# The first load of an average-pooling kernel, in three transfers by partitions

## The chip, the cores and the metric

The kernel runs on one core of a Trainium2 chip. The metric is the device time of one execution in microseconds (us), as the median of several runs. Of the core's engines the kernel uses VectorE (DVE in the profile) for all arithmetic and SyncE (SP) to issue transfers. Transfers are carried by the 16 DMA engines of the core. GpSimd (POOL) only fills a few constants at the start.

## The reference

The input `x` is a float32 array of shape (8, 32, 32, 32, 32): batch, channels, depth, height, width. The result is the mean of each 2 x 2 x 2 window, an array of shape (8, 32, 16, 16, 16). Cut to what matters:

```python
for i in range(out_d):
    for j in range(out_h):
        for k in range(out_w):
            window = x[:, :, 2*i:2*i+2, 2*j:2*j+2, 2*k:2*k+2]
            result[:, :, i, j, k] = np.mean(window, axis=(-3, -2, -1))
```

Every input value is read once: 33.55 MB in, 4.19 MB out.

## The kernel before

Batch and channel make 256 rows of 32,768 values. The first 128 rows are the first half of the work (`t == 0`), one row on each of the 128 partitions. The other 128 rows are the second half (`t == 1`), which is taken as flat memory and cut so that each load is one contiguous region.

`plan` lists ten units: four of 32 KB a partition (4.19 MB each) in the first half, then four of 24 KB and two of 16 KB in the second. For each unit the loop at the end of `pool_rows` takes a tile `tin` from a pool of five buffers, issues its load on SP (line 87) and calls `pool_unit`. There VectorE adds pairs of depth planes (line 68), pairs along the width (line 71) and pairs along the height with the factor 0.125 (line 74), which goes into one of two output buffers `obuf`. Since there are five buffers, the load of unit six waits until VectorE is through with unit one, and so on. [...]

Three stores follow: the first four units of the second half, the whole first half, and the last two units. All stand on SP's queue behind the ten loads.

The second function works on the finished list of instructions. It rewrites the source patterns of the loads of the second half into 64 rows of double length, and those of two stores; the loads of the first half stay as they are, 128 rows with a distance between them. It relaxes the wait of the first store by moving it one VectorE instruction later. Then it takes the first transfer in the list and moves it into the opening block, ahead of the barrier in which all engines meet at the start:

```python
    load = next(i for i in program if isinstance(i, mybir.InstDMACopy))
    ...
    program.remove(load)
    opening.insert(barrier, load)
```

The rest of it rewrites the end of the program, so that SP and not the barrier waits for the semaphores of the stores. A transfer is known to have landed by its semaphore; the framework gives out eight of them to the transfers in turn, and VectorE's first addition of a unit waits for the semaphore of that unit's load.

Of the kernel before, what the change touches and what calls it, by code (L numbers as in the profile page):

```python
# [12 lines left out]
@with_exitstack  # L13
def pool_rows(
    ctx: ExitStack,
    tc: tile.TileContext,
    x: bass.AP,
    kernel_size: int,
    out: bass.AP,
):  # L20
    nc = tc.nc
    assert kernel_size == 2, "only kernel_size == 2 supported"

    B, C, D, H, W = x.shape
    P = nc.NUM_PARTITIONS
    assert (B * C, D, H, W) == (2 * P, 32, 32, 32)
    add = mybir.AluOpType.add

    xv = x.rearrange("b c d h w -> (b c) (d h w)")[:P]
    ov = out.rearrange("b c d h w -> (b c) (d h w)")[:P]
    xf = x.rearrange("b c d h w -> (b c d h w)")[P * 128 * KF:]
    of = out.rearrange("b c d h w -> (b c d h w)")[P * 16 * KF:]

    pool_in = ctx.enter_context(tc.tile_pool(name="pin", bufs=5))
    pool_out = ctx.enter_context(tc.tile_pool(name="pout", bufs=1))
    obuf = [pool_out.tile([P, 16 * KF], F32, name=f"obuf{t}") for t in range(2)]
    dummy = pool_out.tile([P, 1], F32, name="dummy")


    plan = [
        (0, 0, 32),
        (0, 32, 32),
        (0, 64, 32),  # L50
        (0, 96, 32),
        (1, 0, 24),
        (1, 24, 24),
        (1, 48, 24),
        (1, 72, 24),
        (1, 96, 16),
        (1, 112, 16),
    ]

    def pool_unit(buf, t, k0, kb, split):  # L60

        od = kb // 8
        a = buf.rearrange("p (o dd e) -> p o dd e", o=od, dd=2)
        b = buf[:, :od * 1024]
        bv = b.rearrange("p (o e) -> p o e", o=od)
        cuts = (0, 1, od) if split else (0, od)
        for o0, o1 in zip(cuts, cuts[1:]):
            nc.vector.tensor_add(out=bv[:, o0:o1], in0=a[:, o0:o1, 0], in1=a[:, o0:o1, 1])  # L68
        bv = b.rearrange("p (e ww) -> p e ww", ww=2)
        c = buf[:, od * 1024:od * 1536]  # L70
        nc.vector.tensor_add(out=c, in0=bv[:, :, 0], in1=bv[:, :, 1])  # L71
        cv = c.rearrange("p (j hh k) -> p j hh k", hh=2, k=16)
        o0 = k0 * KF // 8
        nc.vector.tensor_tensor_reduce(  # L74
            out=obuf[t][:, o0:o0 + od * 256].rearrange("p (j k) -> p j k", k=16),
            in0=cv[:, :, 0], in1=cv[:, :, 1],
            scale=0.125, scalar=0.0, op0=add, op1=add, accum_out=dummy[:, :],
        )

    for t, k, kb in plan:  # L80
        tin = pool_in.tile([P, 32 * KF], F32, tag="tin", name="tin")
        buf = tin[:, :kb * KF]
        if t == 0:
            src = xv[:, k * KF:(k + kb) * KF]
        else:
            src = xf[P * k * KF:P * (k + kb) * KF].rearrange("(p e) -> p e", p=P)
        nc.sync.dma_start(out=buf, in_=src)  # L87
        pool_unit(buf, t, k, kb, split=k == 96 and t == 1)

    for k, n, kb in [(0, 4, 3), (12, 2, 2)]:
        nc.sync.dma_start(
            out=of[P * k * KF:P * (k + n * kb) * KF].rearrange("(u p e) -> p u e", u=n, p=P),
            in_=obuf[1][:, k * KF:(k + n * kb) * KF].rearrange("p (u e) -> p u e", u=n),
        )
        if k == 0:
            nc.sync.dma_start(out=ov, in_=obuf[0])


def kernel(tc: tile.TileContext, x: bass.AP, kernel_size: int, out: bass.AP):
    nc = tc.nc
    pool_rows(tc, x, kernel_size, out)
    tc.close()
    tc.compile()  # L105
# [123 lines left out]
```

## Time and profile before

| What | Value |
|---|---|
| median of 10 runs | 91.36 us (91.34 to 91.56) |
| the profiled execution | 91.39 us |
| its span, from the first to the last instruction of the program | 86.8 us |
| VectorE busy | 64.5 us, 74% of the span |
| data read and written | 33.55 MB and 4.19 MB |
| loads, stores | 10, 3 |

The span begins with the issue of the first load and ends with the last instruction that belongs to a line of the program. The last store lands after that, so the profiled execution's own time is longer than its span. In the lists below, times are microseconds from the start of the span unless they are marked as ns. L87 is line 87 of the kernel, `SPq` is SP's queue, and "idle before" names what ended an engine's idle time.

### The profile page before, as it was taken

Reading aid. Unit: us, or ns where it says so; the run is one execution under the profiler, and the core shown is the slowest. Engines: PE = TensorE matmul, PEld = TensorE weight load, DVE = VectorE, ACT = ScalarE, POOL = GpSimd, SP = SyncE. Lnnn points to the kernel's source line nnn. Section 1 sums busy time; section 2 is a strip of 40 time slices with the busy share of each in tenths; the row PEclk is TensorE's granted clock in tenths of the full one; section 3 lists DMA queues with packets and bytes.
Section 4 is the critical chain, followed back from the end, with each engine's and each line's share of the span. In section 5 each row is a group of like instructions: output and inputs, shape, how many; then the busy total and the mean of one; then the engine's idle time right before and its main releaser. Section 6 shows DMA issues by size and latency. Waiting matters only on the chain.

```text
span 86.8 us, 91 instructions
## 1 busy us (share of the span) xinstructions
DVE 64.5 (74%) x41; POOL 0.2 (0%) x4
## 2 busy tenths in 40 slices
DVE  0000049992999749992999999799589959999992
POOL 0000000000000000000000000000000000000000
DMA  8889997999979999699889988889988899889999
GB/s 242 378 363 468 483 483 332 393 483 483 483 332 393 483 483 483 302 423 604 363 363 408 657 385 363 363 363 589 499 363 363 363 483 483 378 347 423 431 446 415
DMA packets 1299, 36.75 MB, mean 424 GB/s; under 512 B 176, under 2 KB 176, under 8 KB 176
## 3 DMA queue, kind: packets, MB, share of 16 engines
q1 hardware_dynamic: 1299, 36.75, 99.3%
HBM read 33.55 MB, written 4.19 MB: 435 GB/s over the span
## 4 chain that ended last, share of the span: by engine, by line
DMA 71%; DVE 26%; issue 0%; SPq 0%; DVEq 0%
DMA tin<-in_x_dram 71%; DVE tin L68 14%; DVE tin L71 8%; DVE obuf L74 4%; SPq L87 0%; DVE dummy L74 0%; DVEq L105 0%
## 5 line engine op out<-in xcount | busy, mean ns | idle before, releaser
L68 DVE TENSOR_TENSOR tin<-tin 128x4096 f32<-128x4096 f32 (+3 forms) x11 | 35.9, 3260 | 20.0 <-DMA tin<-in_x_dram 20.0
L71 DVE TENSOR_TENSOR tin<-tin 128x2048 f32<-128x2048 f32 (+2 forms) x10 | 18.7, 1865 | 0.3
L74 DVE CUSTOM_DVE_ANT_1 obuf<-tin 128x1024 f32<-128x1024 f32 (+2 forms) x10 | 10.1, 1012 | 0.3
L74 DVE DVE_READ_ACCUMULATOR2_ANT dummy<- 128x1 f32 x10 | 0.8, 82 | 0.0
L210 POOL MEMSET const-uint8-127<- 128x1 uint8 x1 | 0.1, 102 | 0.0
L210 POOL MEMSET const-bfloat16-1.0<- 128x1 bf16 x1 | 0.1, 101 | 0.0
L210 POOL MEMSET const-float32-0.0<- 128x1 f32 x1 | 0.1, 98 | 0.2 <-issue 0.2
L210 POOL MEMSET const-float32-1.0<- 128x1 f32 x1 | 0.1, 98 | 0.0
## 6 DMA issues: line engine op xcount, KB each, us to landing
tin<-in_x_dram SPq DMA_DIRECT2D x4, 4096.0 KB, 25.7
tin<-in_x_dram SPq DMA_DIRECT2D x4, 3072.0 KB, 34.5
tin<-in_x_dram SPq DMA_DIRECT2D x2, 2048.0 KB, 25.4
out_dram<-obuf SPq DMA_DIRECT2D x1, 2048.0 KB, 10.3
out_dram<-obuf SPq DMA_DIRECT2D x1, 1536.0 KB, 6.1
out_dram<-obuf SPq DMA_DIRECT2D x1, 512.0 KB, 4.8
```

The costliest lines, as they stand in the source:

```text
L68: nc.vector.tensor_add(out=bv[:, o0:o1], in0=a[:, o0:o1, 0], in1=a[:, o0:o1, 1])
L71: nc.vector.tensor_add(out=c, in0=bv[:, :, 0], in1=bv[:, :, 1])
L74: nc.vector.tensor_tensor_reduce(out=obuf[t][:, o0:o0 + od * 256].rearrange("p (j k) -> p j k", k=16), in0=cv[:, :, 0], in1=cv[:, :, 1], s ...
L210: nc = _bacc.Bacc("TRN2", target_bir_lowering=False, num_devices=1)
```

## The change

The load of the first unit is issued as three transfers into the same tile: partitions 0, 4, 8, ..., 124 (32 of them), then 2, 6, 10, ..., 126 (32), then all the odd ones (64). All other loads stay one transfer of 128 partitions. The rewriting of the program is unchanged: it moves the first transfer of the list, which is now the first of the three parts. The other two parts stand behind the barrier, ahead of the load of unit two.

```diff
         else:
             src = xf[P * k * KF:P * (k + kb) * KF].rearrange("(p e) -> p e", p=P)
-        nc.sync.dma_start(out=buf, in_=src)
+        for a, step in ((0, 4), (2, 4), (1, 2)) if t == k == 0 else ((0, 1),):
+            nc.sync.dma_start(out=buf[a:P:step], in_=src[a:P:step])
         pool_unit(buf, t, k, kb, split=k == 96 and t == 1)
```

## The prediction

> **What bounds the kernel now.** I read the page first, then the timeline, then the transfers in a window over the first four microseconds. The page, its first line, its row for VectorE, its account of the transfers and its list of issues:
>
> ```profile
> span 86.8 us, 91 instructions
> ...
> DVE 64.5 (74%) x41; POOL 0.2 (0%) x4
> ...
> DMA  8889997999979999699889988889988899889999
> ...
> HBM read 33.55 MB, written 4.19 MB: 435 GB/s over the span
> ...
> out_dram<-obuf SPq DMA_DIRECT2D x1, 2048.0 KB, 10.3
> out_dram<-obuf SPq DMA_DIRECT2D x1, 1536.0 KB, 6.1
> out_dram<-obuf SPq DMA_DIRECT2D x1, 512.0 KB, 4.8
> ```
>
> To see: the 16 DMA engines are busy in every slice, VectorE three quarters of the time. 37.75 MB must pass. The last column is time from issue to landing. The timeline of the engines:
>
> ```profile
> 12.08 4.43 DVE L68 TENSOR_TENSOR tin<-tin 128x4096 f32<-128x4096 f32 x1 [12.08 <-DMA tin<-in_x_dram]
> ...
> 21.79 4.42 DVE L68 TENSOR_TENSOR tin<-tin 128x4096 f32<-128x4096 f32 x1 [1.69 <-DMA tin<-in_x_dram]
> ...
> 31.51 4.43 DVE L68 TENSOR_TENSOR tin<-tin 128x4096 f32<-128x4096 f32 x1 [1.70 <-DMA tin<-in_x_dram]
> ...
> 41.23 4.42 DVE L68 TENSOR_TENSOR tin<-tin 128x4096 f32<-128x4096 f32 x1 [1.70 <-DMA tin<-in_x_dram]
> ...
> 78.43 0.58 SPq L98 DMA_DIRECT2D out_dram<-obuf  x1
> ...
> 85.21 0.57 SPq L93 DMA_DIRECT2D out_dram<-obuf  x1
> ```
>
> Each unit starts when its load lands, and loads of 4.19 MB land 9.71 us apart: 432 GB/s. The second store, issued at 78.43, lands 10.3 later at 88.7; the last, issued at 85.21, lands 4.8 later at 90.0, that is 1.3 after the one ahead of it. Its 0.52 MB take 1.21 at 432 GB/s, so it queued behind the other and the engines stayed full. The time is therefore a start, then 37.75 MB at the engines' rate (87.4 us), then an end. The profiled execution took 91.39, of which 1.4 lie outside the first issue and the last landing. A change counts if it moves the first data, breaks the flow, or lowers the rate.
>
> The first load landed at 12.08, not 9.71: 2.37 us are the start. The transfers in the window from 0 to 4 us, in 40 slices of 0.1 us, a packet being counted where it begins:
>
> ```profile
> DMA  0000000000999090908000000008979990000000
> GB/s 0 0 0 0 0 0 0 0 0 0 2621 983 655 0 328 0 328 0 328 0 0 0 0 0 0 0 0 328 983 328 983 1966 655 0 0 0 0 0 0 0
> DMA packets 32, 1.05 MB, mean 262 GB/s; under 512 B 0, under 2 KB 0, under 8 KB 0
> ```
>
> 328 in a slice is one packet of 32,768 bytes. Nothing moves for 1.0 us. Then eight engines start in one slice, three, two, and the last three at 1.4, 1.6 and 1.8: mean 1.21 us. The second packets begin between 2.7 and 3.3, mean 3.05. So the first packet of an engine takes 1.84 on average, and 32,768 bytes on 16 engines at 432 GB/s should take 1.21. The excess is 0.63 us, and late starters lose little of it, since all engines reach their second packet together.
>
> [...]
>
> **The change part by part.** (a) The issue ahead of the barrier describes 32 rows instead of 128, so each engine's list is two long and not eight. [...] If the excess is the delay of the first reads, nothing is won. Bounds: 0 to 0.91 us gained. I take half the excess, 0.31, because the last three starters lost little although they too made their first read, so not all of it is a delay of every first read[...].
>
> (b) Two more issues on SP. The issues of the loads on SP's queue, durations in ns as least, median and most, and the waits beside them:
>
> ```profile
> L87 SPq DMA_DIRECT2D tin<-in_x_dram x10: 333/472/567, 0.0 to 55.3; - x10
> L87 SPq EVENT_SEMAPHORE  x5: 17/17/17, 12.1 to 49.8; - x5
> ```
>
> 2 x 0.47 = 0.94 us. Behind them stand loads two to five, issued in 0.78 to 2.72 now, then until about 3.7. Load two is first needed when load one is through the engines, near 11.7, so it keeps some 9 us of cover; without it each issue would cost its 0.47. Parts two and three are issued near 0.8 and 1.2. The first part feeds each engine with two packets, 1.84 + 1.21 from 1.21, to about 4.3. Part two had its own wait of 1.0 us over by 1.8 (the same wait as the first issue, an estimate), so 2.4 us of cover.
>
> (c) Each transfer ends with one more semaphore write per engine. The trace shows no gap of its own there: three consecutive pitches of 9.71 us include it. I put 0.01 us each, 0.02 in all; between 0 and 0.05.
>
> (d) VectorE's first add must wait for three semaphores, and load six, which reuses that buffer, too: at most two more waits of 17 ns on each engine. VectorE idles 1.7 us before each of the next three adds, so this is hidden; bare, it would be 0.03. SP's stands ahead of load six, which is held until 20.1 by VectorE anyway. Semaphores shift round the loads and stores, with no more of them at the end.
>
> (e) If the flow begins x earlier, each landing, the adds behind it and the stores move x earlier together. The last store is issued 3.5 us before the one ahead lands, so a delayed VectorE has over 1 us before the stream runs dry; that delay doesn't arise here.
>
> Sum on the profiled execution: 91.39 - 0.31 + 0.02 = 91.10. The median of the runs is 91.36, 0.03 less: 91.07.
>
> **The rivals.** *The start is latency.* The first packets take as long with two rows as with eight;[...] only 0.02 is added. For it: nothing moves for 1.0 us, most of which is after the issue's 0.375. Against it: late starters lose little. 91.38.
>
> [...] Place: the first 4.19 MB. At half rate they take 19.4 us instead of 9.7: 101.1, and all behind moves along[...]. It decides once these bytes flow below about 412 GB/s, 0.5 us lost. Against it: the later loads read 64 double rows and still run at full rate[...].
>
> *A wait for landing.* The parts interleave in one tile; if the program takes them as overlapping, part two is issued only when part one has landed and part three after that. Two restarts of 2.37 us: 91.38 + 4.7 = 96.1. It decides if one such wait stands on SP. I think interleaved rows are told apart.
>
> *Dry lists.* An engine that finishes its two packets before the next list has reached it pays the first-packet excess again, 0.3 to 1.3 us over two joints: 91.7 to 92.6. It decides if part two arrives after 4.3; the 2.4 us of cover in (b) speak against it.
>
> **How the numbers follow.** A difference up to 0.2%, 0.18 us, is about what measurement can't tell from none. The forecast 0.42 (90.5 to 91.18; its own range), latency 0.32, dry lists 0.09, wait 0.07[...]. Faster 0.42, same 0.32, slower 0.26. The range begins at 90.6, leaving 0.03 of the fast tail, and takes in the same and the dry lists up to 92.6: 0.80. [...]
>
> **What would show it.** Right: in the first 4 us the 16 first packets begin closer together and second packets before 2.7 on average; VectorE's first add at about 11.8, with pitches of 9.71 after it. Latency: first add at 12.1. Dry lists: a gap between 4 and 8 us. Wait: SP's second issue after 4.8. [...] The prediction is wrong if the first add moves later, or moves earlier and the last store doesn't.

## The result and the profile after

The changed kernel takes 92.83 us (median of 9 runs, 91.82 to 93.20) against 91.39 us for the kernel before on the same chip (31 runs, 91.32 to 91.56). From all these runs it is estimated to be 1.0146 times as long, 95% interval 1.0129 to 1.0162. The profiled execution took 92.69, that of the kernel before 91.39.

The page of the changed kernel, the rows that answer to those shown of the kernel before:

```profile
span 88.1 us, 95 instructions
...
DVE 64.5 (73%) x41; POOL 0.2 (0%) x4
...
DMA  7699998999979999979889988898889997996999
...
HBM read 33.55 MB, written 4.19 MB: 429 GB/s over the span
...
out_dram<-obuf SPq DMA_DIRECT2D x1, 2048.0 KB, 10.3
out_dram<-obuf SPq DMA_DIRECT2D x1, 1536.0 KB, 6.1
out_dram<-obuf SPq DMA_DIRECT2D x1, 512.0 KB, 4.8
```

VectorE works as long as before, the stores take as long from issue to landing, the bytes are the same. Only the span is longer, by 1.3. The timeline of the changed kernel says where:

```profile
13.52 4.43 DVE L68 TENSOR_TENSOR tin<-tin 128x4096 f32<-128x4096 f32 x1 [13.52 <-DMA tin<-in_x_dram]
...
23.12 4.43 DVE L68 TENSOR_TENSOR tin<-tin 128x4096 f32<-128x4096 f32 x1 [1.59 <-DMA tin<-in_x_dram]
...
32.83 4.42 DVE L68 TENSOR_TENSOR tin<-tin 128x4096 f32<-128x4096 f32 x1 [1.69 <-DMA tin<-in_x_dram]
...
86.50 0.57 SPq L97 DMA_DIRECT2D out_dram<-obuf  x1
```

The first add is late by 13.52 - 12.08 = 1.44 us. The second is late by 1.33, the third by 1.32, the last store by 86.50 - 85.21 = 1.29. All of the loss is there before the first unit is complete, and the rest of the kernel is the old one, moved. Of the 1.44 at the first add, 0.10 is VectorE's own: its wait for three semaphores is now partly an instruction by itself, at 13.42 in the trace, ahead of the add at 13.52. Since VectorE idles before the second add, this goes no further. The transfers of the changed kernel in the window from 0 to 4 us, 0.1 us a slice:

```profile
DMA  0000000000000999990990700000008999990000
GB/s 0 0 0 0 0 0 0 0 0 0 0 0 0 1311 655 983 655 328 0 655 328 0 328 0 0 0 0 0 0 0 328 655 983 1311 655 1311 0 0 0 0
```

The first packets begin at 1.3 instead of 1.0. The mean of the 16 starts, read from the slices as in the prediction, is 1.64 instead of 1.21; the last is at 2.2 to 2.3. That is the first part of the loss. The second shows in the window from 4 to 6 us, slices of 0.05 us, where a packet of 32,768 bytes counts 655:

```profile
GB/s 0 0 0 0 0 0 0 655 1311 1966 0 655 1311 655 655 1311 1311 0 0 0 0 0 655 0 0 0 0 0 0 0 0 0 1311 655 655 655 1311 1311 1311 655
DMA packets 44, 0.92 MB, mean 459 GB/s; under 512 B 16, under 2 KB 16, under 8 KB 16
```

The 16 small packets, of 4 bytes each, are the ends of part one, one an engine. Fifteen engines begin part two between 4.35 and 4.85. The sixteenth begins at 5.1. Between 5.6 and 6.1 the trace again has only fifteen starts, so the first packet of the late engine also took longer than the others'. The packet records don't name the engines, but only one end of part one, at 4.54, has no packet right behind it. So this engine stands idle for 0.6 us; then its first packet of part two takes 1.88 us, where most of the others take 1.2. The excess of some 0.65 is about that of a first packet at the start of the kernel.

The trace also keeps the 16 increments of each load's semaphore, one an engine. In the kernel before they come within 0.4 us of each other at every load, and so do those of part one here. Of part two, fifteen have come by 7.56 and the last comes at 8.52; of part three, by 12.42 and at 13.39; of the last load, by 80.61 and at 81.49. One engine falls behind where part two follows part one, and every later load waits for it.

SP's issues of the loads in the changed kernel:

```profile
L91 SPq DMA_DIRECT2D tin<-in_x_dram x12: 449/481/942, 0.0 to 56.7; - x12
```

The shortest is 449 ns, where the kernel before had 333.

### The profile page after: what moved, and what is told of

Its sections match the earlier page's. It is cut to its first block, busy times and chain, and to the rows that moved or that the text cites. A ratio compares the mean times of both kernels' runs of the same rounds, so it can differ in the third digit from the quotient of the medians.

```text
span 88.1 us, 95 instructions
## 1 busy us (share of the span) xinstructions
DVE 64.5 (73%) x41; POOL 0.2 (0%) x4
## 3 DMA queue, kind: packets, MB, share of 16 engines
HBM read 33.55 MB, written 4.19 MB: 429 GB/s over the span
## 4 chain that ended last, share of the span: by engine, by line
DMA 69%; DVE 26%; SPq 2%; issue 1%; DVEq 0%
DMA tin<-in_x_dram 69%; DVE tin L68 14%; DVE tin L71 7%; DVE obuf L74 4%; SPq L91 2%; DVE dummy L74 0%; DVEq L109 0%
```

## The experiments

The ratios and differences in time of an experiment are against the kernel before, run again in the same set (91.35 to 91.39 us). A list is what one engine has to carry of one transfer, a joint the place where one list ends and the next begins, and its cover the time by which the next list is there before an engine needs it.

Theory A has two terms. First: an issue of strided partitions is slow. In the program as it is built, the framework puts a mark, `ant_dge_precooked`, on loads of neighbouring partitions like the old first load, and on none of the three parts; the kernel's own line 124 takes it off the loads of the second half. Second: one engine is through with its two packets of part one before its list for part two has reached it, and has to start anew.

Theory B: rows of a strided part are carried more slowly. Theory C: each further transfer costs a start. A2 came later: the late engine is late for a reason of its own, whatever lies ahead of the joint.

### The old first load without the mark

```diff
     program.remove(load)
+    load = copy.replace(load, ant_dge_precooked=False)
     opening.insert(barrier, load)
```

> The kernel before, whole first load, but the mark ant_dge_precooked taken off it; nothing else. Theory A (strided parts lose this mark, and an unmarked issue is slow; then one engine's list runs dry at the joint): the first issue takes 0.55 to 0.60 us instead of 0.375, the first packets begin at 1.2 to 1.4 instead of 1.0, the first add at 12.3 to 12.5, the time is 91.6 to 91.8. Theory B (rows of a strided part are carried more slowly[...]) and theory C (more transfers cost a start each): 91.4, no change.

Measured: 91.70 us, ratio 1.0044 (1.0031 to 1.0057). SP's first instruction in the timeline, of the kernel before, of this one and of the changed kernel in turn:

```profile
0.00 0.38 SPq L87 DMA_DIRECT2D tin<-in_x_dram  x1
```

```profile
0.00 0.58 SPq L87 DMA_DIRECT2D tin<-in_x_dram  x1
```

```profile
0.00 0.59 SPq L91 DMA_DIRECT2D tin<-in_x_dram  x1
```

With 128 rows or with 32, an unmarked first issue takes the same 0.58 to 0.59 us, and here too the first packets begin at 1.3. The first add comes at 12.37, 0.29 late. The mark by itself is worth 0.3 us of the 1.44, and 32 rows instead of 128 are worth nothing in this duration.

### The odd rows first

```diff
-        for a, step in ((0, 4), (2, 4), (1, 2)) if t == k == 0 else ((0, 1),):
+        for a, step in ((1, 2), (0, 4), (2, 4)) if t == k == 0 else ((0, 1),):
```

> The changed kernel with the parts in another order: the 64 odd rows ahead of the barrier, then the two parts of 32. Each engine has four packets ahead of the joint instead of two. Theory A: the slow first issue stays, the late engine is gone: first add at 12.4 to 12.6, 91.7 to 91.9. Theories B and C: as the changed kernel, 92.6 to 93.0.

Measured: 91.80 us (1.0050, 1.0038 to 1.0063), first add at 12.65. The same three transfers, the same slow first issue, but four packets an engine ahead of the first joint instead of two: of the loss of 1.44 us in the median, 0.44 are left. The window from 4 to 8 us, slices of 0.1 us, a packet counting 328:

```profile
GB/s 0 0 0 0 0 1638 1966 983 655 0 0 0 0 0 0 0 0 983 1311 1966 983 0 0 0 0 0 0 0 0 655 1639 1639 983 328 0 0 0 0 0 0
```

At the first joint, now between 6.9 and 7.4, all sixteen engines begin the second transfer together, and the last increment of every load comes within 0.07 us of the one ahead of it. That is theory A; B and C expected the time of the changed kernel.

### The parts in unit two

```diff
-        for a, step in ((0, 4), (2, 4), (1, 2)) if t == k == 0 else ((0, 1),):
+        for a, step in ((0, 4), (2, 4), (1, 2)) if (t, k) == (0, 32) else ((0, 1),):
```

> The first load whole as before; the load of unit two goes in the three strided parts instead, in mid-stream. Theory A: nothing is dry there and no start is late: 91.4 to 91.5. Theory B: the slow rows cost the same 1.0 or so in mid-stream: 92.4. Theory C: between, at most 91.8.

Measured: 91.41 us (1.0006, 1.0000 to 1.0013). The adds of units two and three in the timeline of this kernel:

```profile
21.88 4.42 DVE L68 TENSOR_TENSOR tin<-tin 128x4096 f32<-128x4096 f32 x1 [1.79 <-DMA tin<-in_x_dram]
...
31.47 4.43 DVE L68 TENSOR_TENSOR tin<-tin 128x4096 f32<-128x4096 f32 x1 [1.57 <-DMA tin<-in_x_dram]
```

Unit two's add is 0.09 late, which is the extra wait instruction: its last part lands at 21.75, the whole load landed at 21.77 before. Unit three is on time (31.51 before). In mid-stream the three strided transfers cost at most some 0.1 us: not the shape of the parts and not their number, but where they stand. Theories B and C fall for these parts.

### Three parts by columns

```diff
-        nc.sync.dma_start(out=buf, in_=src)
+        for c0, c1 in ((0, 2048), (2048, 4096), (4096, 8192)) if t == k == 0 else ((0, kb * KF),):
+            nc.sync.dma_start(out=buf[:, c0:c1], in_=src[:, c0:c1])
```

> The first load in three transfers of all 128 partitions, by columns: 8 KB, 8 KB and 16 KB a partition. The same bytes ahead of the barrier and at each joint as in the change, but marked issues and whole partition sets. Theory A: the first issue takes 0.375 again, first packets at 1.0, part two described 0.45 us earlier; 91.2 to 91.6, with a late engine only if two packets' worth of cover is too little by itself. Theory B: 91.4. Theory C: 92.4.

Measured: 91.57 us (1.0021, 1.0012 to 1.0031), in the upper part of what theory A allowed. The marked first issue took 0.38, the first packets began at 1.0, no engine was late by a microsecond, and the first add came at 12.33, 0.25 after that of the kernel before. Nothing was gained here by a smaller first transfer, though its issue was as quick as the old one. Of these 0.25, 0.10 are the extra wait of VectorE; the last part lands at 12.20 instead of 12.05. What these 0.15 us consist of was not tested; the rows are moved in pieces of 8 and 16 KB.

### Sixteen rows first

```diff
-        for a, step in ((0, 4), (2, 4), (1, 2)) if t == k == 0 else ((0, 1),):
+        for a, step in ((0, 8), (4, 8), (2, 4), (1, 2)) if t == k == 0 else ((0, 1),):
```

> The changed kernel with a smaller first part: partitions 0, 8, ..., 120 (16 rows, one packet an engine), then 4, 12, ... (16), then 2, 6, ... (32), then the odd ones (64). Theory A (an engine that is through with its first part before the next list has reached it starts anew): each engine has 1.2 us less of cover, so more engines are late at the joint or one is later; 93.0 to 94.5. A rival, A2 (the late engine is late for a reason of its own, whatever lies ahead of the joint): as the changed kernel, 92.6 to 93.0.

Measured: 94.13 us (1.0294, 1.0281 to 1.0307). The time is in the range that theory A gave, but not for its reason. In the trace all 16 engines, not a late one, take about 2.35 us for each packet of the two parts of 16 rows, and 1.2 for those of the odd rows. An estimate: two parts of 0.52 MB at half rate cost 2.4 us more, and with the 0.35 of the slow issue that is about the whole loss of 2.74. Such a part writes every eighth partition instead of every fourth, and the rows of `x` that it reads lie 1 MiB apart instead of 512 KiB; no run separates the two, so what makes its packets take twice as long was not shown. The run says nothing about the joint.

### Three parts ahead of the barrier

```diff
-    load = next(i for i in program if isinstance(i, mybir.InstDMACopy))
+    heads = [i for i in program if isinstance(i, mybir.InstDMACopy)][:3]
+    load = heads[0]
...
-    program.remove(load)
-    opening.insert(barrier, load)
+    for n, i in enumerate(heads):
+        program.remove(i)
+        opening.insert(barrier + n, i)
```

> The changed kernel with all three parts ahead of the barrier. Part two is issued at about 0.65 instead of 1.23. Theory A: 0.6 us more cover at the joint, and the late engine is gone or rare: 91.7 to 92.2. A2: 92.6 to 93.0. The barrier comes some 1.2 us later and nothing that is needed early stands behind it.

Measured: 91.74 us (1.0041, 1.0025 to 1.0056). The window from 4 to 6 us of this kernel, slices of 0.05 us as above:

```profile
GB/s 0 0 0 0 0 0 655 0 1966 0 656 655 1966 1966 1311 1311 0 0 0 0 0 0 0 0 0 0 0 0 0 0 655 0 1966 0 0 1311 655 3277 1311 655
DMA packets 47, 1.02 MB, mean 508 GB/s; under 512 B 16, under 2 KB 16, under 8 KB 16
```

Now all sixteen engines begin part two between 4.3 and 4.8, and no straggler follows. Parts two and three were issued at 0.64 and 1.26 instead of 1.23 and 1.78; nothing else of them was changed, and load two behind them is issued at 2.50 instead of 2.42. The time is that of the slow first issue alone. So 0.6 us at the issue decide over a whole microsecond of the kernel.

### Contiguous parts

```diff
-        for a, step in ((0, 4), (2, 4), (1, 2)) if t == k == 0 else ((0, 1),):
-            nc.sync.dma_start(out=buf[a:P:step], in_=src[a:P:step])
+        for a, z in ((0, 32), (32, 64), (64, P)) if t == k == 0 else ((0, P),):
+            nc.sync.dma_start(out=buf[a:z], in_=src[a:z])
```

> The changed kernel with contiguous parts: partitions 0 to 31, 32 to 63, 64 to 127. The first two are eligible for the mark that strided parts lose. Theory A: the first issue takes 0.33 to 0.38 again and the first packets begin at 1.0. By itself that would be 91.4 to 92.2. [...]packets of 32,768 bytes take up to 2.4 us instead of 1.21 in the first 10 us, and the time is 93 to 101.

Measured: 101.65 us (1.1120, 1.1105 to 1.1134). The windows of this kernel: begin, end and length, busy time of VectorE and of GpSimd, the clock of an engine that the kernel doesn't use, the busy share of the DMA engines and the rate in GB/s:

```profile
4.00:12.00 8.00, 0.00 (x0) 0.00 (x0) 1.00 0.94 197
12.00:22.00 10.00, 0.00 (x0) 0.00 (x0) 1.00 0.94 210
22.00:32.00 10.00, 7.95 (x4) 0.00 (x0) 1.00 0.97 419
```

The engines are nearly as busy as in the changed kernel (0.94 against 1.02 from 4 to 12 us) and move half as much until the first unit is in: 197 GB/s, mostly into partitions 0 to 63, and 210 into 64 to 127, against 434 in the changed kernel from 4 to 12 us. The first add is at 22.61. The packets of 2.4 us and the 93 to 101 of the expectation were meant for the case that neighbouring rows are carried at half rate, a guess of mine when the run was planned. The rate did halve; why was not shown. The first issue took 0.39, and with 32 marked rows the first packets began at 1.0, just as with 128. So neither the wait nor the issue differs between 32 and 128 rows.

### The changed kernel once more

No edit.

> The changed kernel once more, for a second profile and more times. Theory A: first issue 0.59 and first packets at 1.36 as before; an engine, not always with the same delay, begins the second part late; 92.3 to 93.2, wider spread than the kernel before.

Measured: 92.87 us (92.02 to 93.02; 1.0147, 1.0118 to 1.0175). The window from 4 to 6 us of this execution:

```profile
GB/s 0 0 0 0 0 0 0 0 655 1311 655 1311 1311 1311 655 1311 655 655 0 0 0 0 655 0 0 0 0 0 0 0 0 0 655 0 1311 1311 655 1311 655 1311
```

Again fifteen and one: of part two, the last increment comes 1.08 us after the fifteenth. In both sets of runs one execution is near 91.9 while the others lie at 92.6 and above. That fits an execution without a late engine, but those were not profiled.

### Half the columns first

```diff
-        for a, step in ((0, 4), (2, 4), (1, 2)) if t == k == 0 else ((0, 1),):
-            nc.sync.dma_start(out=buf[a:P:step], in_=src[a:P:step])
+        parts = ((0, 4, 0, 16), (0, 4, 16, 32), (2, 4, 0, 32), (1, 2, 0, 32)) if t == k == 0 else ((0, 1, 0, kb),)
+        for a, step, c0, c1 in parts:
+            nc.sync.dma_start(out=buf[a:P:step, c0 * KF:c1 * KF], in_=src[a:P:step, c0 * KF:c1 * KF])
```

> The changed kernel with its first part cut once more, by columns: partitions 0, 4, ..., 124 with the first 16 KB of their rows ahead of the barrier, their other 16 KB, then the partitions 2, 6, ... and the odd ones as in the change. [...] An engine has 1.2 us less to do ahead of the first joint. Theory A: the late engine becomes several or is later: 93.0 to 94.5. A2 (one engine is late whatever lies ahead): 92.6 to 93.0. If it comes out under 92.3, the cover at the joint is not the cause.

Measured: 93.31 us (1.0237, 1.0209 to 1.0265), as theory A had it and above A2. In the trace the second transfer lands on 12 engines by about 5.0 us and on the other four at 5.5 to 6.3. Less work ahead of the joint makes more engines late; this is what the run with 16 rows was meant to show.

### The same, two transfers ahead of the barrier

```diff
-    load = next(i for i in program if isinstance(i, mybir.InstDMACopy))
+    heads = [i for i in program if isinstance(i, mybir.InstDMACopy)][:2]
+    load = heads[0]
...
-    program.remove(load)
-    opening.insert(barrier, load)
+    for n, i in enumerate(heads):
+        program.remove(i)
+        opening.insert(barrier + n, i)
```

> The same four transfers, the first two of them ahead of the barrier, so that the second is issued at about 0.6 instead of 1.23. Theory A: less late than with one ahead, by up to 0.6: 91.8 to 93.4 and below the run with one ahead. A2: equal to it.

Measured: 92.69 us (1.0160, 1.0141 to 1.0178), 0.6 below the run before it. An earlier second issue helps here as well: the second transfer lands on all engines between 4.62 and 5.26, where it took from 4.54 to 6.28. The third transfer, issued at 1.86, still lands over 1.2 us, from 7.22 to 8.43, so its joint keeps part of the loss.

No run was faster than the kernel before, and none pointed to a version that would be.

## Why the prediction was wrong

*What bounds the kernel* held. The flow is continuous, later pitches stay at 9.71 us (32.83 - 23.12), and what happens to the first load arrives at the end: 1.32 at the third add, 1.29 at the last store. Step (e), that everything behind moves together, is right with the sign reversed.

*Step (a)* failed, and it carried the forecast. It put the gain between 0 and 0.91 us, the excess of 0.63 and three quarters of the 0.375 of the first issue, and took 0.31. That these times shrink with the rows, 32 instead of 128, was an estimate of mine, and no run showed it. The issue got longer, 0.59 instead of 0.38, and the first packets began 0.3 later. Between 32 and 128 rows it does not change: 128 unmarked rows take 0.58, 32 marked ones 0.39. What counted was that a strided part loses the mark, an effect that the bounds left out although line 124 of the kernel handles that very attribute. The excess of 0.63 us in the first packets, which I halved as gain, stayed near that in the runs with packets of 32 KB at full rate: from the first to the second packet of an engine they have 1.7 to 1.9 us on average, the kernel before 1.84. Among unmarked first transfers it is 1.83 with 128 rows, 1.94 with 64 and 1.72 to 1.79 with 32, so it hardly grows with the list, and what it is was not tested.

*Step (b)*, the cover of the joint, failed in size. I reckoned that part two's list reached the engines by 1.8 and was needed at 4.3, 2.4 us of cover. Part two was issued at 1.23, because the barrier comes later behind the slow first issue (SP is through it at 1.15 instead of 0.70); with the wait of 1.3 us that the first packets show, the list would be due near 2.6 and needed from 4.35. There should have been some 1.7 us left, yet one engine went without. That the cover decides is shown by three runs that change little else: 0.6 us more and four packets instead of two each remove the late engine, half the work makes several late. All ten times of the first two lie under 92.0. In the late engine 3.9 us passed between the issue of part two and its first packet; I had reckoned with the 1.0 us of an idle start. That its list was what came late is inferred from these runs, since the trace shows no lists. In the run by columns, with part two marked and issued at 0.78, no engine was late; no run gave part two the mark at 1.23, so whether an unmarked list is also slower to arrive is open.

*The rival of dry lists* was the right one. It named the place, a gap between 4 and 8 us, the price of 0.3 to 1.3 us and the sign; I gave it 0.09. Its price was put on an otherwise unchanged start, hence 91.7 to 92.6. With the slow issue added, 0.3 to 0.4, it reaches 93.0, and 92.83 lies inside. Both terms together: 0.34 from the unmarked issue, and 1.44 - 0.44 = 1.00 between the parts as they are and the odd rows first. At the one joint the late engine lost some 1.25, 0.6 of it idle and 0.65 in a long first packet; the rival had put 0.3 to 1.3 on both joints together.

*The other rivals.* A wait for landing: part two is issued at 1.23 while part one lands at 5.1, so there is none. A lower rate: I gave 0.10 to the case that the parts of the first 4.19 MB run slower, a guess. It did not arise with the parts chosen here: 434 GB/s from 4 to 12 us, and between 6 and 12 us packets mostly of 1.21 us, as before. The price I worked out for half rate, 101.1, is close to what the contiguous parts took, 101.65. Latency: no run shows a gain from a small first transfer, so this rival's view of the gain was right, and only the losses were missing from it.

*Steps (c) and (d)*, two more transfer ends and more waits: the three parts in mid-stream cost 0.05 us in all (interval 0 to 0.12), near the 0.02 counted. The bare cost of VectorE's extra wait was taken from SP's waits of 17 ns and put at 0.03; it is 0.10 here, but hidden, as step (d) has it.

What stays open: why exactly one engine is late and which, and what holds its list back so long.

## What to carry to other kernels

When a stream of transfers is the bound, ask whether the first piece outlasts the time until every engine can go on with the next, not only the issue. Here two packets of 32 KB an engine were too few with the second issue at 1.23 us and enough with it at 0.64; four were enough with it at 1.23. Before a load is cut by partitions, look at what each piece loses: the quick form of the issue (0.59 instead of 0.38 us here), and the rate, where neighbouring rows cost ten microseconds here (101.65), every eighth row over two (an estimate from the 94.13) and every fourth row nothing (434 GB/s from 4 to 12 us). Bound an unknown step on the side of loss as well as on that of gain.

## What was not expected of the hardware

One DMA engine out of 16 lost about a microsecond at a joint that the other fifteen passed without a gap, in both profiled executions of the changed kernel. It was still 0.9 us behind the fifteenth at the last load, so the slowest engine set every landing until then: of the load of unit two the fifteenth increment came at 22.14 and the sixteenth at 23.10, and VectorE's add began at 23.12. And the number of rows in a first transfer, 32 or 128, left its issue as it was (0.39 and 0.38 us marked, 0.59 and 0.58 unmarked); 16 rows, unmarked, were no quicker (0.65).
